# One attention block of a three-block kernel: stick-breaking weights by a running product, the band of biases loaded ahead of the norm, gates left as tanh, sliding output by two additions a step

## The chip, the cores and the metric

One Trainium2 chip, one of its cores. Time is device microseconds of that core for one execution of the whole program, the median of several runs. The trace is of one profiled execution.

## The reference, cut to what matters

Three transformer blocks follow each other on 512 tokens of width 1024. The change lies in the third block. Its two kinds of attention are:

```python
def stick_breaking_attention(q, k, v):          # 8 heads of 64
    z = jnp.einsum('bhqd,bshd->bhqs', qblk, k) * scale
    log_beta = jax.nn.log_sigmoid(z)
    log_1mb = jnp.where(causal, jax.nn.log_sigmoid(-z), 0.0)      # causal: key < query
    suffix = lax.cumsum(log_1mb, axis=3, reverse=True) - log_1mb
    a = jnp.where(causal, jnp.exp(log_beta + suffix), 0.0)
    return jnp.einsum('bhqs,bshd->bqhd', a, v)

def sliding_window_sink_attention(q, k, v, sinks, bias):   # 8 heads, 2 of keys, window 128
    s = jnp.einsum('bnqkgd,bnskd->bnkgqs', qb, kb) * scale + bias
    s = jnp.where(valid, s, -jnp.inf)
    m = jnp.maximum(jnp.max(s, axis=-1, keepdims=True), sink)
    e = jnp.exp(s - m)
    pr = e / (jnp.sum(e, axis=-1, keepdims=True) + jnp.exp(sink - m))
    return jnp.einsum('bnkgqs,bnskd->bnqkgd', pr, vb)

# third_block
h = rmsnorm(x, g_mix)
y_a = stick_breaking_attention(q_a, k_a, v_a) @ w_up_a
y_b = sliding_window_sink_attention(q_b, k_b, v_b, sinks, bias) @ w_up_b
merged = jax.nn.sigmoid(gate_a) * y_a + jax.nn.sigmoid(gate_b) * y_b
x = x + merged @ w_o
```

A stick-breaking weight is beta of its key times the product of (1 - beta) over all keys between it and the query. With r(s) the product of (1 - beta) from key s up to the query, the weight of key s is r(s + 1) - r(s); the sums over logarithms and the running product give the same weights. The bias of the sliding attention depends on the distance alone: 8 heads by 128 distances.

## The kernel before, in words

Activations lie transposed: a tile is 128 features by 512 tokens. Every large product is done in two parts of reduced precision, as three matmuls (high by high, high by low, low by high; lines 172 to 174, `gemm`). Weights come from HBM in units of 128x1024 (`wunit`, line 139): SP issues the load, ACT writes the high half (line 156, `wh`), POOL the low one (line 157, `wl`). `K.gps` gives one of the PSUM banks for such a product, and `K.sigmoid` (line 239) is a tanh on ACT and a tensor_scalar on DVE.

The third block (`block3`) runs in these stages. First the last norm of block 2 is applied to the eight tiles of X while the first three units of the block's own weights are already multiplied (`norm.head`, `norm.evict`); the evicted tiles `mb` are then scaled by the new row statistic R (L1945, L1947). Then, in program order, come the biases: two small loads (`oh`, `rb`), a matmul that picks the bias of each of 128 distances (L1992), a copy into `fr`, a row of 384 that is otherwise -1e30, a write of `fr` to DRAM and a load back (L1999) in which each partition starts one element later, so that a [128, 8, 256] band arises.

The sliding attention runs in 8 steps, 2 groups of 4 heads by 4 blocks of 128 queries. `window_scores` adds the band to the scores, takes maximum, exponential and denominator; `window_mix` transposes the weights on PE, splits them (PTh on ACT, PTl on DVE), multiplies by the values, and joins the two halves of the output, which lie in partitions 0 to 63 and 64 to 127 of PSUM, by one copy and four additions of 64x128 (L2067).

The stick-breaking attention has 8 heads. `stick_scores` computes the scores of the four query blocks of a head (128, 256, 384 and 512 keys) into PSUM, adds a mask, and forms the weights in a tile of 1280 columns: DVE clips the scores into p (L2090), ACT copies them into z (L2091), ACT takes exponential and logarithm of p (L2092, L2093), DVE the maximum with z (L2094), four scans from the last key to the first (L2097), the subtraction z - p (L2100), and ACT the exponential (L2101). `stick_mix` transposes the weights 128 columns at a time (L2110), splits them as above (L1982, L1983) and multiplies (L2112, L2113).

A string lists the order in which the pieces are traced: `ORD3[1] = "SgSMMVSSkqMSvgMSVMvSMgVSMMg"`, where S is the scores of a head, M its mix, V its values, k, q, v projections of two heads, and g a unit of gate and up-projection of the sliding output (`gate_b`). This order gives priorities. A planner at compile time orders each engine's instructions by them and by modelled durations, so a piece of lower priority is moved ahead of one whose inputs it takes for late; on the chip each engine then runs its queue in that order. After the stick stage, the gate stage (lines 2197 to 2206) multiplies the stick-breaking output and merges, and `w3_o` follows.

Of the kernel before, what the change touches and what calls it, by code (L numbers as in the profile page):

```python
# [9 lines left out]
F32 = mybir.dt.float32  # L10
# [9 lines left out]
P = 128  # L20
T = 512
# [11 lines left out]
ORD3 = ("Vkk.qqqkv", "SgSMMVSSkqMSvgMSVMvSMgVSMMg", "v")  # L33
AB = 2
DEEP3 = 1
ZP = 0
JOBS = "k0 q0 a2 v0 k1 q1 a3 v1 k2 q2 a4 v2 k3 q3 a5 v3 k4 q4 v4 k5 q5 v5 z0 g0 k6 q6 z1 v6 g1 k7 q7 z2 v7 g2 z3 g3 z4 g4 z5 g5 a6 z6 g6 a7 z7 g7"
RHP = 20
VTB = 1
# [1872 lines left out]
def block3(K, X, rms, out, norm, es):  # L1912
# [3 lines left out]
    pb = sA.enter_context(tc.tile_pool(name="b3b", bufs=8, side="right", reuse_waits="tile"))  # L1916
    mb_tile = lambda: pb.tile([P, T], F32, tag="mb", name=K.nm("mb"))
    side = Side(K, "pT3", "w3_pe", ExitStack())
    first = [(I["w3_kb"][0], P), (I["w3_vb"][0], P), (I["w3_qb"][0], P), (I["w3_qb"][1], P)][:HD[2]]
    head = [mb_tile() for _ in first]  # L1920
    if norm is not None:
# [39 lines left out]
    def proj(w, scale=None):  # L1961
        ps = K.gemm(K.gps(), gx, K.wunit(w))
        s = K.tmp()
        if scale is None:
            nc.vector.tensor_tensor(s, ps, R, MUL)
        else:
            nc.vector.scalar_tensor_tensor(s, ps, scale, R, op0=MUL, op1=MUL)
        return s
# [14 lines left out]
        nc.vector.tensor_tensor(tl, pt[:, :n], th, SUB)  # L1983
        return th, tl


    oh = pW.tile([32, P], F32, name="oh")
    nc.sync.dma_start(oh, I["onehot"])
    rb = pW.tile([32, 8], F32, name="rb")
    nc.sync.dma_start(rb, I["rel_bias"])  # L1990
    ps = K.ps("pt")
    nc.tensor.matmul(ps[:8, :P], lhsT=rb, rhs=oh, start=True, stop=True)  # L1992
    fr = pW.tile([8, 384], F32, name="fr")
    nc.gpsimd.memset(fr, NEG)
    nc.vector.tensor_copy(fr[:, 127:255], ps[:8, :P])
    scr = tc.dram_tile((8, 384), F32, name="scr")
    nc.sync.dma_start(scr, fr)
    bias = pW.tile([P, 8, 256], F32, name="bias")
    nc.sync.dma_start(bias, bass.AP(tensor=scr.tensor, offset=scr.offset, ap=[[1, P], [384, 8], [1, 256]]))  # L1999

# [49 lines left out]
    def window_mix(kv, i, A, oT):  # L2050
        k0 = max(i - 1, 0)
        nb = 2 if i else 1
        O = K.ps("o")
        for j in range(nb):
            pt = K.ps("pt")
            for h in range(4):
                nc.tensor.transpose(pt[:, h * P:(h + 1) * P], A[:, h, j * P:(j + 1) * P], K.ident)
            th, tl = to_operand(pt, T)
            V = VB[:, (k0 + j) * 2 + kv]
            nc.tensor.matmul(O, lhsT=V, rhs=th, start=j == 0, stop=False)  # L2060
            nc.tensor.matmul(O, lhsT=V, rhs=tl, start=False, stop=j == nb - 1)
        lo = pT.tile([64, T], F32, tag="lo", bufs=1, name=K.nm("lo"))
        nc.scalar.activation(lo, O[64:128], AF.Copy)
        for h in range(4):
            c = slice(h * P, (h + 1) * P)
            e = h % 2
            nc.vector.tensor_tensor(oT[h // 2][e * 64:e * 64 + 64, i * P:(i + 1) * P], O[0:64, c], lo[:, c], ADD)  # L2067

    po_tile = lambda: po.tile([P, T], F32R, tag="o", name=K.nm("oo"))


    AT_Q = {1: 0, 0: 256, 2: 384, 3: 768}

    def stick_scores(pS, q, k):
        kh, kl = k
        z = pS.tile([P, 1280], F32, tag="z", name=K.nm("z"))
        p = pS.tile([P, 1280], F32, tag="p", name=K.nm("p"))
        for blocks in ((1, 0), (2,), (3,)):
            S = K.ps("s")
            for i in blocks:  # L2080
                o = AT_Q[i] - AT_Q[blocks[0]]
                L = (i + 1) * P
                N = max(L, 256)
                ql = q[:, i * P:(i + 1) * P]
                nc.tensor.matmul(S[:, o:o + N], lhsT=ql, rhs=kh[:, :N], start=True, stop=False)
                nc.tensor.matmul(S[:, o:o + N], lhsT=ql, rhs=kl[:, :N], start=False, stop=False)
                nc.tensor.matmul(S[:, o + L - P:o + L], lhsT=K.identb, rhs=strict, start=False, stop=True)
            n = sum((i + 1) * P for i in blocks)
            c = slice(AT_Q[blocks[0]], AT_Q[blocks[0]] + n)
            nc.vector.tensor_scalar(p[:, c], S[:, :n], 40.0, None, op0=MIN)  # L2090
            nc.scalar.activation(z[:, c], S[:, :n], AF.Copy)  # L2091
        nc.scalar.activation(p, p, AF.Exp)  # L2092
        nc.scalar.activation(p, p, AF.Ln, bias=K.eps[1.0])  # L2093
        nc.vector.tensor_tensor(p, p, z, MAX)  # L2094
        for i in range(4):
            c = slice(AT_Q[i], AT_Q[i] + (i + 1) * P)
            nc.vector.tensor_tensor_scan(p[:, c][:, ::-1], K.eps[1.0].to_broadcast([P, (i + 1) * P]), p[:, c][:, ::-1], 0.0, MUL, ADD)  # L2097
        for e, a, b in ((nc.gpsimd, 0, ZP), (nc.vector, ZP, 1280)):
            if a < b:
                e.tensor_tensor(z[:, a:b], z[:, a:b], p[:, a:b], SUB)  # L2100
        nc.scalar.activation(z, z, AF.Exp)  # L2101
        return z

    def stick_mix(A, V, e, oT):
        O = K.ps("o")
# [12 lines left out]
    ob = []  # L2118
    mb = []

    def gate_b(u):
        sb = [K.sigmoid(proj(I["w3_gb"][2 * u + j])) for j in range(2)]
        w = K.wunit(I["w3_upb"][u])
        for j in range(2):
            ps = K.gemm(K.gps(), ob, w, off=j * 512)
            t = mb_tile()
            nc.vector.tensor_tensor(t, sb[j], ps, MUL)
            mb.append(t)

    q3, k3, v3, V3, Z, oa, oTs = {}, {}, {}, {}, {}, [], {}  # L2130
# [21 lines left out]
    def stick_out(h):  # L2152
        m, e = divmod(h, 2)
        if not e:
            oTs[m] = pT.tile([P, T], F32, tag="oT", bufs=2, name=K.nm("oT"))
        stick_mix(Z.pop(h), V3[m], e, oTs[m])
        if e:
            oa.append(K.split(oTs[m], None, po_tile))
# [13 lines left out]
    fill = list(ORD3[0])  # L2172
    for n, (kv, i) in enumerate(steps):
        if i == 0:
            oT = [pT.tile([P, T], F32, tag="oT", bufs=2, name=K.nm("oT")) for _ in range(2)]
        if n == 1:
            wq[1] = window_queries(1)
        if n + DEEP3 < 8:
            ahead.append(window_scores(*steps[n + DEEP3], wq[steps[n + DEEP3][0]]))
        window_mix(kv, i, ahead.pop(0), oT)  # L2180
        if i == 3:
            ob += [K.split(oT[m], None, po_tile) for m in range(2)]
        if n >= 3 and fill:
            o = fill.pop(0)
            if o != ".":
                next(todo[o])
    for o in fill:
        next(todo[o])
    sW.close()
    pS = sT.enter_context(tc.tile_pool(name="b3s", bufs=2, reuse_waits="tile"))  # L2190
    for o in ORD3[1]:
        next(todo[o])
    sT.close()
# [3 lines left out]
    for u in range(4):  # L2197
        w = K.wunit(I["w3_upa"][u], 1024, pm)
        for j in range(2):
            m = 2 * u + j  # L2200
            sa = K.sigmoid(proj(I["w3_ga"][m]))
            ps = K.gemm(K.gps(), oa, w, off=j * 512)
            t = K.tmp()
            nc.vector.tensor_tensor(t, sa, ps, MUL)
            nc.vector.tensor_tensor(t, t, mb[m], ADD)
            mg.append(K.split(t, None, lambda: pm.tile([P, T], F32R, tag="mg", bufs=16, name=K.nm("mg"))))
    rms = Rms(K, X, "g_mlp", "R4")
    for m in range(NT):
        ps = K.gemm(K.gps(), mg, K.wunit(I["w3_o"][m]))
# [78 lines left out]
```

## Time and profile before

| | us |
|---|---|
| median of 3 runs (2864.78 to 2866.42) | 2865.03 |
| the profiled execution's own time | 2863.77 |
| its span, first to last instruction | 2862.0 |
| PE busy | 2656.5 (93%) |
| DVE busy | 1764.7 (62%) |
| ACT busy | 1305.6 (46%) |
| POOL busy | 1370.3 (48%) |

The engines are PE (TensorE; PEld is its weight load), DVE (VectorE), ACT (ScalarE), POOL (GpSimd) and SP, which issues DMAs. Of the span, the third block takes what comes after about 2040 us: sliding attention to about 2156, stick-breaking attention to about 2325, the merging of the gates to 2395, then the output projection, the MLP and the side input. Engine times overlap, so a busy time is no share of the end-to-end time by itself. PEclk is the mean clock that TensorE was granted in a stretch, as a share of full speed. In a list of waits, an engine's idle time ahead of an instruction is put down to the instruction whose end released it.

### The profile page before, as it was taken

What the parts mean: (1) busy time and instruction counts of PE and PEld (TensorE: products, weight loads), DVE (VectorE), ACT (ScalarE), POOL (GpSimd) and SP (SyncE); (2) the same over time, 40 slices, a digit from 0 to 9 for tenths busy, and PEclk for the clock granted to TensorE, in tenths of its full rate; (3) what the DMA queues carried; (4) which work ended last, traced back from release to release, by engine and by line L of the source; (5) the groups of instructions that cost most, each with busy time, mean ns of one, the idle gap of its engine ahead of it and who ended that gap; (6) DMA issues with size and microseconds to landing.
All of it is one profiled execution on the core that took longest, in us unless ns stands there. A gap on an engine that the chain in (4) does not pass through costs nothing.

```text
span 2862.0 us, 34137 instructions
## 1 busy us (share of the span) xinstructions
PE 2656.5 (93%) x12206; PEld 2126.7 (74%) x12206; DVE 1764.7 (62%) x2731; ACT 1305.6 (46%) x2375; POOL 1370.3 (48%) x1049
## 2 busy tenths in 40 slices
PE   6899999699999988999989999999889799999997
PEld 5677776478888866777777788887667678788886
DVE  7889898975342496987854711136887765322256
ACT  3357776433222355666534533333556642332234
POOL 6554442454454455644536544454644344444442
PEclk9999999799999999999999999999999899999998
DMA  3321111132222222322322222232322122222222
GB/s 116 114 89 40 62 46 38 53 117 94 95 99 95 97 97 86 105 80 79 101 64 82 78 93 95 96 118 81 118 67 74 38 88 88 96 96 94 94 95 102
DMA packets 81497, 247.52 MB, mean 86 GB/s; under 512 B 11568, under 2 KB 15576, under 8 KB 81328
## 3 DMA queue, kind: packets, MB, share of 16 engines
q1 hardware_dynamic: 81328, 245.35, 26.5%
q8 instruction: 96, 1.57, 0.2%
q14 instruction: 73, 0.60, 0.1%
HBM read 233.06 MB, written 6.62 MB: 84 GB/s over the span
## 4 chain that ended last, share of the span: by engine, by line
PE 67%; DVE 22%; ACT 5%; issue 3%; DMA 1%; POOL 1%; SPq 0%; DVEq 0%; ACTq 0%; POOLq 0%
PE pg L173 19%; PE pg L172 19%; PE pg L174 19%; DVE p L2097 1%; DVE py L733 1%; DVE Zt L1543 1%; DVE X L396 1%; DVE Z L1544 1%; PE ppt L1016 1%; DMA B<-diag 1%; PE ps L994 1%; DVE ln L337 1%; POOL wl L157 1%; PE po L1022 1%; ACT wh L156 1%
## 5 line engine op out<-in xcount | busy, mean ns | idle before, releaser
L157 POOL TENSOR_TENSOR wl<-wst,wh 128x512 fp32r<-128x512 f32 (+1 forms) x808 | 1099.9, 1367 | 1312.7 <-ACT wh L156 1231.6
L156 ACT ACTIVATE wh<-wst 128x512 fp32r<-128x512 f32 (+1 forms) x808 | 500.4, 627 | 964.4 <-PE pg L173 834.9
L172 PE MATMUL pg<-op,wh 128*128 128x512 f32 (+1 forms) x2008 | 813.7, 406 | 36.4 <-ACT wh L156 19.5
L173 PE MATMUL pg<-op,wh 128*128 128x512 f32 (+1 forms) x2008 | 799.6, 398 | 6.2 <-DVE op L192 6.0
L174 PE MATMUL pg<-op,wl 128*128 128x512 f32 (+1 forms) x2008 | 798.1, 398 | 3.9 <-POOL wl L157 3.9
L172 PEld LDWEIGHTS pg<-op,wh 128*128 128x128 f32 (+1 forms) x2008 | 385.7, 192 | 115.7 <-ACT wh L156 20.2
L173 PEld LDWEIGHTS pg<-op,wh 128*128 128x128 f32 (+1 forms) x2008 | 385.5, 192 | 84.6 <-DVE op L192 8.7
L174 PEld LDWEIGHTS pg<-op,wl 128*128 128x128 f32 (+1 forms) x2008 | 384.1, 191 | 86.3 <-POOL wl L157 7.4
L172 PE MATMUL pg<-hid,wh 128*128 128x512 f32 x688 | 272.2, 396 | 0.8 <-DVE hid L191 0.8
L174 PE MATMUL pg<-hid,wl 128*128 128x512 f32 x688 | 272.2, 396 | 0.0
L173 PE MATMUL pg<-hid,wh 128*128 128x512 f32 x688 | 271.8, 395 | 0.2 <-DVE hid L192 0.2
L733 DVE SCALAR_TENSOR_TENSOR py<-z,vec,py 128x512 f32<-128x512 f32 x240 | 180.3, 751 | 10.9 <-ACT py L731 6.2
L1180 DVE TENSOR_TENSOR X<-X,pg 128x512 f32<-128x512 f32 x56 | 38.6, 689 | 222.1 <-PE pg L174 222.1
L172 PEld LDWEIGHTS pg<-hid,wh 128*128 128x128 f32 x688 | 129.1, 188 | 32.8 <-DVE hid L191 1.2
L173 PEld LDWEIGHTS pg<-hid,wh 128*128 128x128 f32 x688 | 129.1, 188 | 32.0 <-DVE hid L192 0.5
L174 PEld LDWEIGHTS pg<-hid,wl 128*128 128x128 f32 x688 | 129.1, 188 | 31.5 <-issue 0.2
L191 DVE CAST hid<-t 128x512 fp32r<-128x512 f32 x86 | 53.1, 617 | 145.5 <-ACT t L1157 144.7
L1171 DVE SCALAR_TENSOR_TENSOR t<-pg,R 128x512 f32<-128x512 f32 x32 | 22.1, 692 | 84.0 <-PE pg L174 83.9
L998 ACT ACTIVATE P<-ps,s 128x128 f32<-128x128 f32 (+3 forms) x128 | 66.5, 524 | 11.6 <-DVE s L997 9.4
L192 DVE TENSOR_TENSOR hid<-t,hid 128x512 fp32r<-128x512 f32 x86 | 63.6, 740 | 3.0
L997 DVE TENSOR_REDUCE s<-ps 128x1 f32<-128x128 f32 (+3 forms) x128 | 60.2, 483 | 8.0 <-PE ps L996 6.8
L1020 DVE TENSOR_TENSOR PTl<-ppt,PTh 128x512 fp32r<-128x512 f32 x80 | 53.4, 685 | 4.7 <-ACT PTh L1019 4.1
(546 smaller groups left out, 4420.3 us busy)
## 6 DMA issues: line engine op xcount, KB each, us to landing
wst<-in_w_f_dram SPq DMA_DIRECT2D x64, 512.0 KB
wst<-in_w_up_dram SPq DMA_DIRECT2D x32, 512.0 KB
wst<-in_w_down_dram SPq DMA_DIRECT2D x32, 512.0 KB
wst<-in_w_ga_dram SPq DMA_DIRECT2D x24, 512.0 KB
wst<-in_w_fg_dram SPq DMA_DIRECT2D x22, 512.0 KB
wst<-in_w_fu_dram SPq DMA_DIRECT2D x22, 512.0 KB
wst<-in_w_q_dram SPq DMA_DIRECT2D x16, 512.0 KB
wst<-in_w_out_dram SPq DMA_DIRECT2D x16, 512.0 KB
```

Source lines behind the costliest of these rows:

```text
L156: nc.scalar.activation(h, st, AF.Copy)
L157: nc.gpsimd.tensor_tensor(l, st, h, SUB)
L172: self.nc.tensor.matmul(ps, lhsT=wh, rhs=h[:, sl], start=first and k == 0, stop=False)
L173: self.nc.tensor.matmul(ps, lhsT=wh, rhs=l[:, sl], start=False, stop=False)
L174: self.nc.tensor.matmul(ps, lhsT=wl, rhs=h[:, sl], start=False, stop=last and k == n - 1)
L191: nc.vector.tensor_copy(h, src)
L192: nc.vector.tensor_tensor(l, src, h, SUB)
L733: nc.vector.scalar_tensor_tensor(y, z[:, k:k + T], w(k), y, op0=MUL, op1=ADD)
L997: nc.vector.tensor_reduce(mx[:, h:h + 1], S[:, :L], AX, MAX, negate=True)
L998: nc.scalar.activation(Pt[h][:, :L], S[:, :L], AF.Exp, bias=mx[:, h:h + 1], accum_out=den[:, h:h + 1])
L1020: nc.vector.tensor_tensor(tl, pt, th, SUB)
L1180: nc.vector.tensor_tensor(X[:, m], X[:, m], ps, ADD)
```

## The change

In `stick_scores`, ACT writes t = tanh(-score/2) from PSUM straight into a tile `tz`, and 0.5 + 0.5 t, which is 1 - beta, into `om`. The query blocks now lie 257, 385 and 513 columns apart in a tile of 1284: each block has one column more, where `tz` holds -1 (so `om` holds 0) and a constant tile `anew` holds 1. One scan over all columns from the last to the first computes r = om * r + anew, which starts again at 1 at each such column. The weights are the differences of neighbouring columns, one subtraction into `A`. `tz` and `om` have one buffer each, `A` has two; before, z and p had two each. The clip, the copy, the maximum, the exponentials and the logarithm are gone.

The band of biases up to its write to DRAM is moved to the top of `block3`, ahead of the norm's head, with its tiles in another pool and its product in the bank group "m". The load of the band stays where it was.

The gates stay tanh: the product with the up-projection becomes (tanh + 1) * y in one scalar_tensor_tensor, and the factor of a half goes into the split of the merged tile. In `window_mix` the output tile of a group holds two 512-column halves, and two additions of 64x(2x128) stand for four of 64x128; the stick-breaking output uses the same kind of tile.

```diff
--- before.py
+++ after.py
@@ -33,7 +33,6 @@
 ORD3 = ("Vkk.qqqkv", "SgSMMVSSkqMSvgMSVMvSMgVSMMg", "v")
-ZP = 0
...
 RHP = 20
 VTB = 1
@@ -1916,6 +1915,18 @@
     pb = sA.enter_context(tc.tile_pool(name="b3b", bufs=8, side="right", reuse_waits="tile"))
     mb_tile = lambda: pb.tile([P, T], F32, tag="mb", name=K.nm("mb"))
     side = Side(K, "pT3", "w3_pe", ExitStack())
+
+    oh = pb.tile([32, P], F32, tag="oh", bufs=1, name="oh")
+    nc.sync.dma_start(oh, I["onehot"])
+    rb = pb.tile([32, 8], F32, tag="rb", bufs=1, name="rb")
+    nc.sync.dma_start(rb, I["rel_bias"])
+    ps = K.ps("m")
+    nc.tensor.matmul(ps[:8, :P], lhsT=rb, rhs=oh, start=True, stop=True)
+    fr = pb.tile([8, 384], F32, tag="fr", bufs=1, name="fr")
+    nc.gpsimd.memset(fr, NEG)
+    nc.vector.tensor_copy(fr[:, 127:255], ps[:8, :P])
+    scr = tc.dram_tile((8, 384), F32, name="scr")
+    nc.sync.dma_start(scr, fr)
     first = [(I["w3_kb"][0], P), (I["w3_vb"][0], P), (I["w3_qb"][0], P), (I["w3_qb"][1], P)][:HD[2]]
     head = [mb_tile() for _ in first]
     if norm is not None:
@@ -1983,18 +1994,6 @@
         nc.vector.tensor_tensor(tl, pt[:, :n], th, SUB)
         return th, tl
 
-
-    oh = pW.tile([32, P], F32, name="oh")
-    nc.sync.dma_start(oh, I["onehot"])
-    rb = pW.tile([32, 8], F32, name="rb")
-    nc.sync.dma_start(rb, I["rel_bias"])
-    ps = K.ps("pt")
-    nc.tensor.matmul(ps[:8, :P], lhsT=rb, rhs=oh, start=True, stop=True)
-    fr = pW.tile([8, 384], F32, name="fr")
-    nc.gpsimd.memset(fr, NEG)
-    nc.vector.tensor_copy(fr[:, 127:255], ps[:8, :P])
-    scr = tc.dram_tile((8, 384), F32, name="scr")
-    nc.sync.dma_start(scr, fr)
     bias = pW.tile([P, 8, 256], F32, name="bias")
     nc.sync.dma_start(bias, bass.AP(tensor=scr.tensor, offset=scr.offset, ap=[[1, P], [384, 8], [1, 256]]))
 
@@ -2061,45 +2060,47 @@
             nc.tensor.matmul(O, lhsT=V, rhs=tl, start=False, stop=j == nb - 1)
         lo = pT.tile([64, T], F32, tag="lo", bufs=1, name=K.nm("lo"))
         nc.scalar.activation(lo, O[64:128], AF.Copy)
-        for h in range(4):
-            c = slice(h * P, (h + 1) * P)
-            e = h % 2
-            nc.vector.tensor_tensor(oT[h // 2][e * 64:e * 64 + 64, i * P:(i + 1) * P], O[0:64, c], lo[:, c], ADD)
+        pair = lambda t, e: t.rearrange("p (m e k) -> p m e k", m=2, e=2)[:, :, e]
+        for e in range(2):
+            nc.vector.tensor_tensor(oT[e * 64:e * 64 + 64, :, i * P:(i + 1) * P], pair(O[0:64], e), pair(lo, e), ADD)
 
     po_tile = lambda: po.tile([P, T], F32R, tag="o", name=K.nm("oo"))
 
 
-    AT_Q = {1: 0, 0: 256, 2: 384, 3: 768}
+
+    AT_Q = {1: 0, 0: 257, 2: 386, 3: 771}
+    NZ = 1284
+    ends = [AT_Q[i] + (i + 1) * P for i in range(4)]
+    anew = pT.tile([P, NZ], F32, bufs=1, name="anew")
+    nc.gpsimd.memset(anew, 0.0)
+    for c in ends:
+        nc.gpsimd.memset(anew[:, c:c + 1], 1.0)
+    half = pT.tile([P, 1], F32, bufs=1, name="half")
+    nc.gpsimd.memset(half, 0.5)
 
     def stick_scores(pS, q, k):
         kh, kl = k
-        z = pS.tile([P, 1280], F32, tag="z", name=K.nm("z"))
-        p = pS.tile([P, 1280], F32, tag="p", name=K.nm("p"))
+
         for blocks in ((1, 0), (2,), (3,)):
             S = K.ps("s")
             for i in blocks:
-                o = AT_Q[i] - AT_Q[blocks[0]]
+                o = 256 * (i == 0)
                 L = (i + 1) * P
                 N = max(L, 256)
                 ql = q[:, i * P:(i + 1) * P]
                 nc.tensor.matmul(S[:, o:o + N], lhsT=ql, rhs=kh[:, :N], start=True, stop=False)
                 nc.tensor.matmul(S[:, o:o + N], lhsT=ql, rhs=kl[:, :N], start=False, stop=False)
                 nc.tensor.matmul(S[:, o + L - P:o + L], lhsT=K.identb, rhs=strict, start=False, stop=True)
-            n = sum((i + 1) * P for i in blocks)
-            c = slice(AT_Q[blocks[0]], AT_Q[blocks[0]] + n)
-            nc.vector.tensor_scalar(p[:, c], S[:, :n], 40.0, None, op0=MIN)
-            nc.scalar.activation(z[:, c], S[:, :n], AF.Copy)
-        nc.scalar.activation(p, p, AF.Exp)
-        nc.scalar.activation(p, p, AF.Ln, bias=K.eps[1.0])
-        nc.vector.tensor_tensor(p, p, z, MAX)
-        for i in range(4):
-            c = slice(AT_Q[i], AT_Q[i] + (i + 1) * P)
-            nc.vector.tensor_tensor_scan(p[:, c][:, ::-1], K.eps[1.0].to_broadcast([P, (i + 1) * P]), p[:, c][:, ::-1], 0.0, MUL, ADD)
-        for e, a, b in ((nc.gpsimd, 0, ZP), (nc.vector, ZP, 1280)):
-            if a < b:
-                e.tensor_tensor(z[:, a:b], z[:, a:b], p[:, a:b], SUB)
-        nc.scalar.activation(z, z, AF.Exp)
-        return z
+            for i in blocks:
+                o = 256 * (i == 0)
+                L = (i + 1) * P
+                nc.scalar.activation(tz[:, AT_Q[i]:AT_Q[i] + L], S[:, o:o + L], AF.Tanh, scale=-0.5)
+        om = pS.tile([P, NZ], F32, tag="om", bufs=1, name=K.nm("om"))
+        A = pS.tile([P, NZ], F32, tag="A", name=K.nm("A"))
+        nc.scalar.activation(om, tz, AF.Identity, scale=0.5, bias=half)
+        nc.vector.tensor_tensor_scan(om[:, ::-1], om[:, ::-1], anew[:, ::-1], 0.0, MUL, ADD)
+        nc.vector.tensor_tensor(A[:, :NZ - 1], om[:, 1:], om[:, :NZ - 1], SUB)
+        return A
 
     def stick_mix(A, V, e, oT):
         O = K.ps("o")
@@ -2118,13 +2119,18 @@
     ob = []
     mb = []
 
+    def half_gate(s):
+
+        nc.scalar.activation(s, s, AF.Tanh, scale=0.5)
+        return s
+
     def gate_b(u):
-        sb = [K.sigmoid(proj(I["w3_gb"][2 * u + j])) for j in range(2)]
+        sb = [half_gate(proj(I["w3_gb"][2 * u + j])) for j in range(2)]
         w = K.wunit(I["w3_upb"][u])
         for j in range(2):
             ps = K.gemm(K.gps(), ob, w, off=j * 512)
             t = mb_tile()
-            nc.vector.tensor_tensor(t, sb[j], ps, MUL)
+            nc.vector.scalar_tensor_tensor(t, sb[j], 1.0, ps, op0=ADD, op1=MUL)
             mb.append(t)
 
     q3, k3, v3, V3, Z, oa, oTs = {}, {}, {}, {}, {}, [], {}
@@ -2152,7 +2158,9 @@
     def stick_out(h):
         m, e = divmod(h, 2)
         if not e:
-            oTs[m] = pT.tile([P, T], F32, tag="oT", bufs=2, name=K.nm("oT"))
+            if not m % 2:
+                oTs["two"] = pT.tile([P, 2, T], F32, tag="oT2", bufs=1, name=K.nm("oT"))
+            oTs[m] = oTs["two"][:, m % 2]
         stick_mix(Z.pop(h), V3[m], e, oTs[m])
         if e:
             oa.append(K.split(oTs[m], None, po_tile))
@@ -2172,14 +2180,14 @@
     fill = list(ORD3[0])
     for n, (kv, i) in enumerate(steps):
         if i == 0:
-            oT = [pT.tile([P, T], F32, tag="oT", bufs=2, name=K.nm("oT")) for _ in range(2)]
+            oT = pT.tile([P, 2, T], F32, tag="oT2", bufs=1, name=K.nm("oT"))
         if n == 1:
             wq[1] = window_queries(1)
         if n + DEEP3 < 8:
             ahead.append(window_scores(*steps[n + DEEP3], wq[steps[n + DEEP3][0]]))
         window_mix(kv, i, ahead.pop(0), oT)
         if i == 3:
-            ob += [K.split(oT[m], None, po_tile) for m in range(2)]
+            ob += [K.split(oT[:, m], None, po_tile) for m in range(2)]
         if n >= 3 and fill:
             o = fill.pop(0)
             if o != ".":
@@ -2188,6 +2196,9 @@
         next(todo[o])
     sW.close()
     pS = sT.enter_context(tc.tile_pool(name="b3s", bufs=2, reuse_waits="tile"))
+    tz = pS.tile([P, NZ], F32, bufs=1, name="tz")
+    for c in ends:
+        nc.gpsimd.memset(tz[:, c:c + 1], -1.0)
     for o in ORD3[1]:
         next(todo[o])
     sT.close()
@@ -2198,12 +2209,12 @@
         w = K.wunit(I["w3_upa"][u], 1024, pm)
         for j in range(2):
             m = 2 * u + j
-            sa = K.sigmoid(proj(I["w3_ga"][m]))
+            sa = half_gate(proj(I["w3_ga"][m]))
             ps = K.gemm(K.gps(), oa, w, off=j * 512)
             t = K.tmp()
-            nc.vector.tensor_tensor(t, sa, ps, MUL)
+            nc.vector.scalar_tensor_tensor(t, sa, 1.0, ps, op0=ADD, op1=MUL)
             nc.vector.tensor_tensor(t, t, mb[m], ADD)
-            mg.append(K.split(t, None, lambda: pm.tile([P, T], F32R, tag="mg", bufs=16, name=K.nm("mg"))))
+            mg.append(K.split(t, 0.5, lambda: pm.tile([P, T], F32R, tag="mg", bufs=16, name=K.nm("mg"))))
     rms = Rms(K, X, "g_mlp", "R4")
     for m in range(NT):
         ps = K.gemm(K.gps(), mg, K.wunit(I["w3_o"][m]))
```

## Rows read from the trace of the kernel before

**Rows 1.** The page, its head and part 1: busy us, share, instructions

```profile
span 2862.0 us, 34137 instructions
...
PE 2656.5 (93%) x12206; PEld 2126.7 (74%) x12206; DVE 1764.7 (62%) x2731; ACT 1305.6 (46%) x2375; POOL 1370.3 (48%) x1049
```

**Rows 2.** Stage table: us, length, PE, PEld, DVE, ACT, POOL busy (count), PEclk, DMA

```profile
2060.00:2100.00 40.00, 33.35 (x145) 26.18 (x144) 24.87 (x54) 17.47 (x42) 23.25 (x19) 0.87 0.36 113
2100.00:2156.00 56.00, 49.15 (x237) 36.48 (x236) 50.24 (x121) 32.44 (x89) 22.42 (x17) 1.00 0.22 67
...
2156.00:2340.00 184.00, 157.31 (x722) 124.44 (x721) 133.18 (x164) 111.97 (x164) 76.54 (x51) 0.93 0.20 63
...
2340.00:2395.00 55.00, 55.00 (x244) 45.43 (x243) 32.76 (x45) 14.96 (x26) 24.77 (x18) 1.00 0.29 96
```

**Rows 3.** Waits, 2156 to 2340 us: engine, line, releaser: total us, times, longest

```profile
POOL wl L157 <- ACT wh L156: 104.0, 23, 14.2
...
PE po L2113 <- DVE PTl L1983: 11.1, 6, 4.9
...
PE ppt L2110 <- ACT z L2101: 9.6, 4, 4.7
...
ACT z L2091 <- DVE p L2090: 8.0, 4, 4.1
...
PE ps L2085 <- ACT z L2091: 5.1, 2, 2.7
```

**Rows 4.** Groups by line, 2156 to 2340 us: busy, mean ns, idle before

```profile
L2097 DVE TENSOR_TENSOR_SCAN p<-eps,p 128x128 f32<-128x128 f32 (+3 forms) x32 | 41.0, 1342 | 0.1
L2090 DVE TENSOR_SCALAR p<-ps 128x384 f32<-128x384 f32 (+1 forms) x24 | 13.9, 594 | 9.7 <-PE ps L2087 9.7
L2091 ACT ACTIVATE z<-ps 128x384 f32<-128x384 f32 x16 | 7.3, 494 | 6.9 <-DVE p L2090 6.8
L2091 ACT ACTIVATE z<-ps 128x512 f32<-128x512 f32 x8 | 4.8, 594 | 1.3 <-DVE p L2090 1.2
L2093 ACT ACTIVATE p<-p,eps 128x1280 f32<-128x1280 f32 x8 | 10.9, 1367 | 0.1
L2093 ACT ACT_TABLE_LOAD x8 | 10.3, 1283 | 0.1
L242 ACT ACT_TABLE_LOAD x4 | 5.1, 1283 | 0.1
L2101 ACT ACT_TABLE_LOAD x4 | 5.1, 1283 | 0.1
L2101 ACT ACTIVATE z<-z 128x1280 f32<-128x1280 f32 x8 | 10.2, 1271 | 28.0 <-DVE z L2100 28.0
L2094 DVE TENSOR_TENSOR p<-p,z 128x1280 f32<-128x1280 f32 x8 | 11.9, 1490 | 9.4 <-ACT p L2093 9.4
L2100 DVE TENSOR_TENSOR z<-z,p 128x1280 f32<-128x1280 f32 x8 | 14.3, 1790 | 0.0
L244 DVE TENSOR_SCALAR t<-t 128x512 f32<-128x512 f32 x9 | 8.2, 916 | 9.4 <-ACT t L242 9.4
```

**Rows 5.** Order in time, DVE: start, us, line, form; two neighbouring heads' four scans

```profile
2230.07 3.97 DVE L2097 TENSOR_TENSOR_SCAN p<-eps,p 128x128 f32<-128x128 f32 x4
...
2246.17 7.07 DVE L2097 TENSOR_TENSOR_SCAN p<-eps,p 128x128 f32<-128x128 f32 x4
```

**Rows 6.** Order in time, 2059 to 2076 us: POOL, DVE, PE

```profile
2059.76 0.41 POOL L1994 MEMSET fr<- 8x384 f32 x1
...
2061.13 2.36 DVE L1945 TENSOR_TENSOR mb<-mb,R 128x512 f32<-128x512 f32 x2
...
2063.84 0.58 PE L1992 MATMUL ppt<-oh,rb 32*8 32x128 f32 x2 [2.88 <-DMA rb<-in_rel_bias_dram]
...
2075.41 0.42 DVE L2030 TENSOR_TENSOR A<-ps,bias 128x256 f32<-128x256 f32 x1 [2.98 <-DMA bias<-scr]
```

**Rows 7.** Groups by line, 2060 to 2156 us: the four additions of a step

```profile
L2067 DVE TENSOR_TENSOR oT<-po,lo 64x128 f32<-64x128 f32 x32 | 9.0, 282 | 2.2 <-ACT lo L2063 1.8
```

## The prediction

> **What bounds the kernel now.** I read the page's engine totals first: PE is busy 2656.5 of 2862.0 us, a share no other engine comes near [rows 1]. So a change is worth what it takes out of PE's idle time and out of the time in which PE's clock is granted low. Then the stage table (columns: stretch, its length, busy time of PE, PEld, DVE, ACT, POOL with counts, granted clock, DMA share, GB/s) finds where the touched code runs. The stick-breaking stage, 2156 to 2340 us, is 184.0 us long and PE is busy in only 157.31 of it at a mean clock of 0.93; the gate stage after it (2340 to 2395) is PE from end to end at 1.00; the two stretches ahead (2060 to 2100, 2100 to 2156) hold the band of biases and the sliding attention [rows 2]. In the stick stage PE therefore loses 184.0 - 157.31 = 26.7 us standing and, by the clock, some 0.07 x 184 = 12.9 us running in part at the lower of its two levels (1.2 and 2.4 GHz): 39.6 us is all that can be had there.
>
> The list of waits says what PE stood for [rows 3]: 11.1 us for PTl, DVE's low halves of the transposed weights; 9.6 us for the finished weights z; 5.1 us for score banks that ACT and DVE had not yet read. These three make 25.8 of the 26.7 us. The reader is to see that every one ends at DVE or ACT work of one head, and that DVE (133.18 of 184) and ACT (111.97) are far from full: it is latency in order, not throughput. The groups by line then give each instruction's price [rows 4], and the order in time shows the scans: a head's four take 3.97 us in one place and 7.07 us in another [rows 5].
>
> **The change part by part: stick_scores.** Eight heads. Removed on ACT: copies 7.3 + 4.8 us in all, two exponentials of 128x1280 a head (row of one; the other has its form) 2 x 10.2, the logarithm 10.9, and table loads 10.3 + 5.1 + 5.1 = 20.5 us, which go because tanh, identity and copy need no change of table here: tanh at L242 loads one only after a logarithm. Together 63.9 us [rows 4]. Added: four tanh a head from PSUM. A 384-wide read costs 494 ns and a 512-wide 594, so 100 ns per 128 columns, and 128 to 512 sum to 0.29 + 0.39 + 0.49 + 0.59 = 1.78 us. One identity of 1284 columns with a tile as bias, priced by the logarithm that has one too, 1.37. Eight times 3.15 is 25.2 us. ACT falls by 38.7, from 112 to 73 us.
>
> Removed on DVE: the clip 13.9, the maximum 11.9, the scans 41.0, the subtraction 14.3 us. Added: one scan of 1284 columns and one subtraction. The scan has the same two operations per element as before; its first operand is now a full tile in place of a broadcast column, a form that no row shows at this size. Bounds: 3.97 us, the undisturbed four [rows 5], and 7.07; I take the mean of before, 41.0 / 8 = 5.13. The subtraction lies between 1.49 and 1.79 (the maximum's and the old subtraction's means). So 8 x (5.13 + 1.79) = 55.3 us stand for 81.1, and nine of the gates' DVE steps (L244, 8.2 us) go in this stage: DVE falls by 34, from 133 to 99 us.
>
> Per head the chain from scores to weights was 1.27 + 1.28 + 1.37 + 1.49 + 5.13 + 1.79 + 1.27 = 13.6 us and becomes 1.37 + 5.13 + 1.79 = 8.3: shorter by 5.3, while the longest single wait for z is 4.7 [rows 3]. On PE's instructions nothing changes.
>
> What of PE's 26.7 us goes? The score banks: the slot is now given back by ACT alone, and ACT had waited 8.0 us for the clip on DVE [rows 3]; 5.1 becomes 0.5. The wait for z: in an unchanged order of PE all of it would go; but the compiler's planner writes a new order against the shorter chain and will put the transposes earlier, so I leave 3.5 of 9.6 (bounds 0 and 9.6). The wait for PTl: PTl queues on DVE behind the next head's scan, and the scan stays. The longest, 4.9, is the one behind the 7.07 us scan and I cut it to 2.0; the other 6.2 I leave at 5.5. So 7.5 of 11.1 (bounds 3 and 11.1). With 0.6 of small ones PE stands 12.1 us, 14.6 less. The low clock follows standing in this stage, 12.9 / 26.7 = 0.48 us per us: 7.1 more. Stage: -21.7 us. What is late next is PTl behind the scan.
>
> On that scan the trace shows 3.97 us where POOL runs little and 7.07 where POOL's splits run beside it [rows 5]. The Trainium skill, SBUF — State Buffer, section Who interferes with whom, says that a DVE instruction with two SBUF inputs and a GpSimd instruction that reads SBUF exclude each other for a whole instruction. By that rule one long scan is held off once rather than up to four times, so its price is nearer the lower bound, and DVE would save up to 8 x 1.16 = 9.3 us more, which is mostly off the path; it also means that POOL is held for a whole scan, which is the last rival below.
>
> **The gates.** Sixteen tensor_scalar steps on DVE go; the factor of a half moves into the split of the merged tile, and the added one rides on the product that reads PSUM anyway. In the gate stage PE has no gap [rows 2], so this is worth nothing there; in the stick stage it is counted above. Were the products dearer by as much as the removed step (0.92), that would give back 8 us of DVE's 34 and still be covered by DVE's idle time.
>
> **The band of biases.** PE stands 2.88 us for its two small loads and then runs the 0.58 us product; but the transposes behind it need the second of two evicted tiles, ready at 2061.13 + 2.36 = 2063.49, only 0.35 before that product starts at 2063.84 [rows 6]. So the old place yields 0.35 + 0.58 us, not 3.4, and the product's 0.58 is paid again where it goes. All of it is issued again ahead of the norm: two loads, a write to DRAM and the memset pass the queues of SP and POOL there, the product and a copy those of PE and DVE. The write waits on SP for the copy, with the next weight loads queued behind it. If PE stood for the loads there as it does here, 2.9 is lost. DVE's 2.98 us wait for the band at 2075.41 goes [rows 6], but DVE is busy only 24.87 of 40 us in that stretch [rows 2]. I take -0.5 (bounds -2.9 and +2.6).
>
> **The sliding output.** 32 additions of 0.282 [rows 7] become 16 of 256 columns; the 256-column addition out of PSUM takes 0.42 [rows 6]: 9.0 becomes 6.7, in a stretch where DVE is busy 50.24 of 56 us and PE 49.15. Of the 2.3 us I take 1.0 on the path (bounds 0 and 2.3). **New memsets:** ten on POOL, one of 1284 columns; by the 384-column one, 0.41 [rows 6], 1.4 us and at most 0.41 for each other. Six of them, 3.4 us, fall where POOL is busy 23.25 of 40 [rows 2]; I take +0.5 (bounds 0 and 3.4).
>
> **Sum.** -21.7 - 0.5 - 1.0 + 0.5 = -22.7 from the profiled execution's 2863.77 (span 2862.0 and 1.77 around it): 2841.1. The median shown, 2865.03, lies 1.26 above it, so 2842.
>
> **Rivals.** *PE runs dense.* For it: DVE at 99 and ACT at 73 us are far under PE's 157. Against: the order on PE is fixed when the kernel is built and the scan stays. All 39.6 and 1.5 elsewhere go: 2824. *Only the banks.* The new plan pulls the transposes ahead as far as the chain got shorter, and the waits for z and PTl stay: 4.6 x 1.48 = 6.8 and 1.0 elsewhere: 2857. *It doesn't save what it says:* the plan gives back every gap, or the scan over two full tiles costs what the removed steps did (81.1 / 8 = 10.1 us a head less the subtraction's 1.79, so a scan of 8.3): 2865. *The single om buffer, slower.* om was two tiles p; now the identity of a head waits for the subtraction of the head before, and behind it on ACT's queue stand the splits of weights, PTh and tanh, for which PE waits. Held for scan and subtraction, 5.5 us, on seven heads, it costs 7 x 5.5 x 1.48 = 57: 2899; it turns the result above the old time from 22.7 / 1.48 / 7 = 2.2 us a head. It decides if two heads' scores come less than 5.5 us apart; before, two neighbours' scans start 16.1 apart [rows 5]. *POOL held by the long scan.* Weight splits come up to 3.97 us later for each of eight heads: 8 x 3.97 x 1.48 = 47, so 2889; against it, POOL idles 104.0 us of this stage waiting for ACT [rows 3], and PE's large waits name no split.
>
> **How the numbers follow.** Forecast 0.55 (its own range 2832 to 2852), dense 0.14, only the banks 0.15, nothing saved 0.08, om 0.05, POOL 0.03. About 0.2% (5.7 us) is what can be told from no change: faster 0.55 + 0.14 + 0.15 = 0.84, same 0.08, slower 0.08. The range, 2822 to 2859, takes in the first three.
>
> **What would show it.** Right: no table load between 2156 us and the stage's end, one scan a head of 4 to 5.5 us, the stage near 162 us, PE's longest wait there PTl behind a scan, next to none for score banks. Wrong: waits for A above 6 us in sum (the plan), a scan above 7 us with POOL idle, ACT waiting for DVE ahead of the identity, or PE waiting for wl.

## The result, and the profile after

The changed kernel takes 2834.23 us (median of 4 runs, 2831.8 to 2839.88) against 2865.33 us: the ratio is 0.9895 (95% interval 0.9881 to 0.991). On another chip, beside the last experiments, it was 0.992 (0.9901 to 0.9939), 2838.68 against 2862.52 us. So the change is worth 24 to 31 us, and the forecast, 2842 us with 22.7 us taken off, lies just under that. Single runs of one kernel lay up to 20 us apart (the band alone: 2854.22 to 2873.77; the kernel before on that chip: 2854.99 to 2869.82), so differences under some 4 us between experiments are not read.

The profiled execution of the changed kernel is the fastest of the first four, 2831.8 us, and 6.0 us of its lead over the profile of before had arisen by the last addition of block 2 (1947.0 and 1953.0 us), before the first instruction that the edits move or add (2003.9). Over all fourteen profiles of this case that addition starts anywhere from 1946.4 to 1958.9 us. Stages are therefore compared by their lengths. From the first column sum of the third block's norm to the first addition of the output projection the kernel before needs 344.8 us (2052.7 to 2397.5) and the changed one 316.6 (2048.5 to 2365.1), 28.2 less. What follows takes 464.5 and 464.9 us. This stretch leaves out what the moved band costs ahead of the column sum (below). Counted from the last addition of block 2, the kernel before needs 444.46 us up to the same end and the changed one 418.13, 26.33 less. The change's lines are one less than before up to the third block, so L156 here is L157 there.

The page's head and part 1 of the changed kernel, to set against [rows 1]:

```profile
span 2830.0 us, 34046 instructions
...
PE 2644.3 (93%) x12206; PEld 2119.3 (75%) x12206; DVE 1712.2 (61%) x2643; ACT 1269.2 (45%) x2351; POOL 1366.0 (48%) x1059
```

The stage table, its borders moved to the same pieces of work (columns as in [rows 2]):

```profile
2055.00:2095.00 40.00, 33.30 (x147) 26.48 (x146) 24.98 (x51) 18.23 (x43) 24.14 (x19) 0.87 0.32 103
2095.00:2150.00 55.00, 47.73 (x233) 35.90 (x232) 49.37 (x107) 31.80 (x87) 23.07 (x21) 1.00 0.23 68
2150.00:2306.00 156.00, 146.82 (x716) 116.03 (x715) 86.55 (x98) 75.68 (x140) 76.28 (x51) 0.99 0.24 75
2306.00:2361.00 55.00, 55.00 (x244) 45.45 (x243) 27.64 (x36) 14.47 (x25) 24.20 (x18) 1.00 0.28 95
```

The stick stage is 156 us long in place of 184. PE stands 9.2 us of it, not 26.7, and its clock is granted at 0.99, not 0.93. The stages ahead of it and the gate stage are as long as they were. The waits of PE and ACT between 2150 and 2325 us (columns as in [rows 3]):

```profile
PE po L2114 <- DVE PTl L1994: 5.9, 6, 2.9
...
PE po L2113 <- DVE VA L1988: 1.9, 1, 1.9
...
ACT om L2100 <- DVE A L2102: 1.3, 2, 1.0
...
PE po L2113 <- DVE oT L2117: 0.6, 1, 0.6
PE ps L2091 <- ACT tz L2097: 0.5, 1, 0.5
```

The wait of PE for finished weights is gone, that for score banks is 0.5, and that for PTl is about halved. The groups of the new instructions (columns as in [rows 4]; there is no table load among them):

```profile
L2101 DVE TENSOR_TENSOR_SCAN om<-om,anew 128x1284 f32<-128x1284 f32 x8 | 23.4, 2922 | 9.3 <-ACT om L2100 9.3
L2102 DVE TENSOR_TENSOR A<-om 128x1283 f32<-128x1283 f32 x8 | 16.7, 2092 | 0.1
L2100 ACT ACTIVATE om<-tz,half 128x1284 f32<-128x1284 f32 x8 | 11.0, 1373 | 1.4 <-DVE A L2102 1.3
...
L2133 DVE SCALAR_TENSOR_TENSOR mb<-t,pg 128x512 f32<-128x512 f32 x8 | 5.5, 688 | 16.9 <-PE pg L173 16.9
...
L2097 ACT ACTIVATE tz<-ps 128x512 f32<-128x512 f32 x8 | 4.7, 590 | 1.7 <-PE ps L2093 1.6
```

One scan takes 2.92 us in the mean, where four took 5.13 [rows 4]. The band of biases, in the order in time of DVE and PE (compare [rows 6]):

```profile
2056.74 2.31 DVE L1956 TENSOR_TENSOR mb<-mb,R 128x512 f32<-128x512 f32 x2
...
2059.20 1.09 PE L1985 MATMUL ppt<-ident,mb 128*128 128x128 f32 x4 [3.59 <-DVE mb L1956]
...
2069.12 0.41 DVE L2029 TENSOR_TENSOR A<-ps,bias 128x256 f32<-128x256 f32 x1
```

DVE no longer waits for the band, and PE no longer for its loads; PE now stands 3.59 us at the same place for the evicted tiles. Counted from the column sum (2052.66 and 2048.50 us), the transposes there start 1.0 us earlier, at 10.70 us in place of 11.70. But time is lost ahead of the column sum. From the last addition of block 2 to it the changed kernel needs 101.5 us, the kernel before 99.6. The waits of PE in that part, first in the changed kernel and then before (columns as in [rows 3]):

```profile
PE pg L171 <- ACT o L1805: 2.9, 1, 2.9
PE pg L171 <- DVE ln L431: 2.7, 1, 2.7
PE pm L412 <- POOL wl L156: 1.3, 1, 1.3
```

```profile
PE pm L413 <- POOL wl L157: 3.3, 1, 3.3
PE pg L172 <- DVE ln L432: 0.9, 1, 0.9
```

The wait of 2.9 us for `o`, a copy out of PSUM by ACT, stands in the traces of all six kernels that have the band moved, which need 100.4 to 102.6 us there. It stands in none of the eight others, which need 99.6 to 99.8. How the moved instructions bring it about was not taken apart.

### The profile page after: what moved, and what is told of

Read it like the earlier page. It is cut to its first block, busy times and chain, and to the rows that moved or that the text cites. A ratio compares the mean times of both kernels' runs of the same rounds, so it can differ in the third digit from the quotient of the medians.

```text
span 2830.0 us, 34046 instructions
## 1 busy us (share of the span) xinstructions
PE 2644.3 (93%) x12206; PEld 2119.3 (75%) x12206; DVE 1712.2 (61%) x2643; ACT 1269.2 (45%) x2351; POOL 1366.0 (48%) x1059
## 4 chain that ended last, share of the span: by engine, by line
PE 70%; DVE 19%; ACT 5%; issue 2%; POOL 1%; DMA 1%; SPq 0%; DVEq 0%; ACTq 0%; POOLq 0%
PE pg L172 20%; PE pg L171 20%; PE pg L173 20%; DVE py L732 1%; DVE Zt L1542 1%; DVE Z L1543 1%; PE ppt L1015 1%; DVE X L395 1%; PE piv L1568 1%; PE ps L993 1%; DVE ln L336 1%; POOL wl L156 1%; PE po L1021 1%; ACT wh L155 1%; ACT P L997 1%
## 5 line engine op out<-in xcount | busy, mean ns | idle before, releaser
L156 POOL TENSOR_TENSOR wl<-wst,wh 128x512 fp32r<-128x512 f32 (+1 forms) x808 | 1094.1, 1360 | 1277.4 <-ACT wh L155 1201.1
```

The source lines that it names most:

```text
L156: nc.gpsimd.tensor_tensor(l, st, h, SUB)
```

## The experiments

All ran beside the kernel before; "stretch" is the one of 344.8 us above, from each kernel's own profile, and the last column counts from the last addition of block 2, as the 444.46 us above. Ratios are to the kernel before of the same chip: the first four rows are from one chip, the next four from a second, the last four from a third.

| | ratio (95% interval) | stretch, us | from block 2, us |
|---|---|---|---|
| stick_scores alone | 0.9914 (0.9897 to 0.9932) | 318.3 | 417.9 |
| band alone | 1.0005 (0.9992 to 1.0019) | 340.6 | 441.6 |
| gates alone | 0.9982 (0.997 to 0.9995) | 336.5 | 436.2 |
| two additions alone | 1.0009 (0.9999 to 1.0018) | 341.8 | 441.6 |
| before, one scan | 0.9962 (0.9947 to 0.9977) | 335.8 | 435.5 |
| changed, table loads back | 0.9913 (0.9899 to 0.9927) | 318.8 | 419.2 |
| before, gates in place | 0.9998 (0.9987 to 1.0009) | 342.0 | 441.7 |
| stick_scores and gates | 0.9919 (0.9906 to 0.9933) | 317.0 | 416.8 |
| changed again | 0.992 (0.9901 to 0.9939) | 313.6 | 416.2 |
| changed, no two additions | 0.9917 (0.9898 to 0.9936) | 316.7 | 418.2 |
| changed, band in its old place | 0.9915 (0.9898 to 0.9931) | 318.0 | 417.6 |
| changed, four scans | 0.9928 (0.991 to 0.9946) | 323.0 | 424.2 |

Three kernels whose time is that of the kernel before (band alone, two additions alone, gates in place) need 441.6 to 441.7 us from block 2 on, 2.7 to 2.9 less than the one profile of the kernel before. So some 3 us of the 26.33 are owed to that profile, and the 24 us of the third chip are the better figure for the change.

**Each edit alone.** Each of the first four takes one part of the diff shown above onto the kernel before.

> The kernel before with the new stick_scores alone (tanh, one scan, one subtraction). Theory (the shorter chain of a head takes PE's waits away): 24 to 28 us under the kernel before, near 2839, the stage from 2156 us on about 24 us shorter, no table load in it. Rival (the gain needs DVE's relief by the gates and the two additions too): at most 15 us, above 2850.

> The kernel before with the band of biases moved ahead of the norm, alone. Theory: PE's wait for the two loads was almost wholly hidden by the wait for the evicted tiles behind it, so 0 to 2 us faster. Rival (the wait of 2.9 us and DVE's wait of 3.0 us for the band were both on the path): 3 to 6 us faster. Other rival (queues ahead of the norm): slower by 1 us or more.

> The kernel before with the gates left as tanh, alone. Theory: nothing in the gate stage, where PE has no gap, and up to 2 us in the stick stage, where nine steps of 0.9 us leave DVE's queue: 0 to 2 us faster. Rival (DVE's queue is the bound of the stick stage): 5 us or more faster.

> The kernel before with two additions a step and the two-half output tile, alone. Theory: 1 us faster (0 to 2.3). Rival (one buffer in place of two holds the next group back): slower by 1 us or more.

stick_scores alone is 24.4 us faster (2838.53 against 2862.97), inside what its theory expected: the gain needs no other edit. The band and the two additions show nothing; the additions' 1 us of the forecast can't be seen, and at 1.0009 their interval leaves 0.3 us of gain at most. The gates alone are 5.1 us faster (2857.91), more than the theory's 2, though the interval (1.4 to 8.6 us) reaches down into it. In their trace the wait for PTl is as before, that for z is 10.7 us against 9.6, and only that for score banks has gone, from 5.1 to 0.6 us (waits of PE, columns as in [rows 3]):

```profile
PE po L2113 <- DVE PTl L1983: 11.1, 6, 4.9
PE ppt L2110 <- ACT z L2101: 10.7, 3, 4.8
PE ps L2085 <- ACT z L2091: 0.6, 2, 0.3
```

**Why the gates help alone.** Two causes were possible, fewer steps on DVE or fewer temporary tiles. The second was tried by itself:

```diff
-        sb = [K.sigmoid(proj(I["w3_gb"][2 * u + j])) for j in range(2)]
+        # gate(s): tanh and tensor_scalar both in place
+        sb = [gate(proj(I["w3_gb"][2 * u + j])) for j in range(2)]
```

> The kernel before with the gates' tanh and tensor_scalar done in place, so that a gate holds one temporary tile and not two; DVE's step stays. Theory (temporary tiles were scarce): 3 to 6 us faster, as the gates left as tanh. Rival (DVE's sixteen steps were the gain): no change within 2 us.

At 0.9998 the tiles give nothing that can be seen (the interval leaves 3.7 us at most). What is left is DVE's sixteen steps, which fits the wait for banks that went but was not tried by itself. On top of stick_scores the gates give nothing (0.9919 with, 0.9914 without, on two chips): with stick_scores alone the wait for banks is already 0.5 us.

**What in stick_scores: the scan.** The kernel before with one scan per head, all else as it was:

```diff
-        for i in range(4):
-            c = slice(AT_Q[i], AT_Q[i] + (i + 1) * P)
-            nc.vector.tensor_tensor_scan(p[:, c][:, ::-1], K.eps[1.0].to_broadcast([P, (i + 1) * P]), p[:, c][:, ::-1], 0.0, MUL, ADD)
+        nc.vector.tensor_tensor_scan(p[:, ::-1], keep[:, ::-1], p[:, ::-1], 0.0, MUL, ADD)   # keep: 1, and 0 at each block's end
```

> The kernel before with its four scans of a head made one of 1280 columns, reset at the block ends by a tile of ones and zeros; clip, logarithm, maximum and exponentials stay. Theory A (a scan is held off by at most one POOL instruction of about 1 us, so four pay up to four times): the scan 2.8 to 3.6 us in place of a mean of 5.1, DVE 12 to 18 us less in the stage, and 6 to 12 us faster. Theory B (the gain comes from the ACT part of the chain): the scan is as short, but at most 4 us faster.

It is 11.3 us faster (2851.45 against 2862.76; interval 6.6 to 15.2 us): theory A. The scan's durations (ns, least, median, greatest) beside those of before, of all widths:

```profile
L2100 DVE TENSOR_TENSOR_SCAN p<-keep,p x8: 2815/3418/3906, 2177.0 to 2306.4; 128x1280 f32<-128x1280 f32 x8
```

```profile
L2097 DVE TENSOR_TENSOR_SCAN p<-eps,p x32: 415/1192/2276, 2172.3 to 2314.5; 128x128 f32<-128x128 f32 x8, 128x256 f32<-128x256 f32 x8, 128x384 f32<-128x384 f32 x8, 128x512 f32<-128x512 f32 x8
```

Why, is seen in the kernel before scan by scan, first the head of 2230 us and then that of 2246, of which [rows 5] gives the lengths (there the four records overlap by some 0.08 us each, so singly they add up to more). In time the order is 128, 256, 384, 512 columns; the lists are sorted by duration:

```profile
L2097 DVE TENSOR_TENSOR_SCAN p<-eps,p 128x128 f32<-128x128 f32 x1 | 1.4, 1427 | 0.0
L2097 DVE TENSOR_TENSOR_SCAN p<-eps,p 128x512 f32<-128x512 f32 x1 | 1.2, 1191 | 0.0
L2097 DVE TENSOR_TENSOR_SCAN p<-eps,p 128x384 f32<-128x384 f32 x1 | 0.9, 926 | 0.0
L2097 DVE TENSOR_TENSOR_SCAN p<-eps,p 128x256 f32<-128x256 f32 x1 | 0.7, 659 | 0.0
```

```profile
L2097 DVE TENSOR_TENSOR_SCAN p<-eps,p 128x512 f32<-128x512 f32 x1 | 2.2, 2223 | 0.0
L2097 DVE TENSOR_TENSOR_SCAN p<-eps,p 128x384 f32<-128x384 f32 x1 | 2.0, 1978 | 0.0
L2097 DVE TENSOR_TENSOR_SCAN p<-eps,p 128x256 f32<-128x256 f32 x1 | 1.7, 1712 | 0.0
L2097 DVE TENSOR_TENSOR_SCAN p<-eps,p 128x128 f32<-128x128 f32 x1 | 1.4, 1386 | 0.0
```

What POOL did meanwhile (start, us, instruction):

```profile
2229.93 1.29 POOL L157 TENSOR_TENSOR wl<-wst,wh 128x512 fp32r<-128x512 f32 x1 [5.35 <-ACT wh L156]
2233.25 1.87 POOL L157 TENSOR_TENSOR wl<-wst,wh 128x512 fp32r<-128x512 f32 x1 [2.03 <-ACT wh L156]
...
2245.97 2.67 POOL L157 TENSOR_TENSOR wl<-wst,wh 128x512 fp32r<-128x512 f32 x2 [7.00 <-ACT wh L156]
2248.85 3.30 POOL L157 TENSOR_TENSOR wl<-wst,wh 128x512 fp32r<-128x512 f32 x2 [0.21 <-ACT wh L156]
```

At 2230.07 one split on POOL is running as the first scan starts, and that scan is long; no split runs as the other three start. At 2246 each of the four scans starts while a split runs, and all four are long. So it is for all 32 scans of this trace. The 14 that start with no POOL instruction running are still (415, 659, 926, 1191 ns for 128 to 512 columns at the shortest). The 18 that start while one runs are longer, 15 of them by 0.97 to 1.09 us (2223 - 1191 = 1032, 1978 - 926 = 1052, 1712 - 659 = 1053, 1386 - 415 = 971) and three by 0.50 to 0.63. In all 18 the excess is the rest of the running POOL instruction, less 0.11 to 0.14 us. So a scan is not slowed, it is held off until that instruction ends, whatever its own width. Four scans can pay four times, and one pays once. POOL is held in turn: a split of 1.29 us beside a still DVE takes 1.87 us when it starts during a scan, as at 2233.25, and up to 3.7 us beside the scan of the changed kernel.

**The scan from the other side.** The changed kernel with its scan cut in four over the same tiles:

```diff
-        nc.vector.tensor_tensor_scan(om[:, ::-1], om[:, ::-1], anew[:, ::-1], 0.0, MUL, ADD)
+        for i in range(4):
+            c = slice(AT_Q[i], ends[i] + 1)
+            nc.vector.tensor_tensor_scan(om[:, c][:, ::-1], om[:, c][:, ::-1], anew[:, c][:, ::-1], 0.0, MUL, ADD)
```

> The changed kernel with its one scan of a head cut into four of 129 to 513 columns over the same two tiles. Theory A (each scan is held off by a POOL instruction of its own): the four take 3.2 us where POOL is still and up to 7 where it runs, 4 to 5 in the mean in place of 2.9, and PE's wait for PTl grows; 4 to 10 us slower than the changed kernel. Rival (the full tile as first operand is what is fast): 3.2 to 3.4 in the mean, within 3 us.

```profile
L2103 DVE TENSOR_TENSOR_SCAN om<-om,anew 128x513 f32<-128x513 f32 x8 | 11.7, 1462 | 0.0
L2103 DVE TENSOR_TENSOR_SCAN om<-om,anew 128x385 f32<-128x385 f32 x8 | 9.6, 1198 | 0.0
L2103 DVE TENSOR_TENSOR_SCAN om<-om,anew 128x257 f32<-128x257 f32 x8 | 6.4, 798 | 0.0
L2103 DVE TENSOR_TENSOR_SCAN om<-om,anew 128x129 f32<-128x129 f32 x8 | 5.2, 651 | 10.1 <-ACT om L2100 10.1
```

The mean of four is 32.9 / 8 = 4.1 us, theory A's lower edge; the full tile as first operand is not what makes it fast. Seven of the 32 scans are held off here, 18 of 32 in the kernel before. One more starts while POOL has a split under way and is not held off: that split began during the scan just ahead and ended 1.1 us after this one, so it was the split that waited. The stretch is 323.0 us, 6 to 9 more than the two profiles of the changed kernel. PE's wait for PTl hardly grows (6.5 us), that for VA does (3.8). By the runs it is 4.1 us slower than the changed kernel (2842.77 and 2838.68), theory A's lower edge again, but the intervals overlap: the profiles support the sign, the size is open.

**What in stick_scores: the table loads.** The changed kernel with two loads ahead of each head's identity:

```diff
+        K.table("natural_log_exp_and_others")
+        K.table("exp_and_others")
         nc.scalar.activation(om, tz, AF.Identity, scale=0.5, bias=half)
```

> The changed kernel with two table loads ahead of the identity of each head: 16 x 1.28 = 20.5 us of ACT back, in the chain of a head. Theory B (ACT's part of the chain): 6 to 14 us slower than the changed kernel, 16 to 24 under the kernel before. Rival (PE is now covered by other work): within 4 us of the changed kernel.

The waits of PE in the same part of its trace:

```profile
PE po L2116 <- DVE PTl L1994: 7.9, 6, 3.9
PE pg L173 <- POOL wl L156: 1.0, 1, 1.0
PE po L2115 <- DVE oT L2119: 0.8, 1, 0.8
PE po L2115 <- ACT PTh L1993: 0.7, 2, 0.4
```

With all 20.5 us of ACT back the ratio is 0.9913; the changed kernel's was 0.9895 on the first chip and 0.992 beside the later experiments. Stick_scores with the gates, on the same chip as this run, has 0.9919. The stretch grows by 2 to 5 us, and no wait for finished stick weights returns. So in the changed kernel the loads cost little, and theory B (ACT's part of the chain) falls for them there. What taking them out was worth in the kernel before, whose chain is longer, no run shows.

**Undoing the rest.** Stick_scores with the gates alone had come out at 0.9919, which against the first chip's 0.9895 looked as if the band and the additions were worth 7 us after all. So the changed kernel was run again, on a third chip, beside versions without the one and without the other.

> The changed kernel without the moved band and without the two additions: stick_scores and gates alone. Theory (the other two edits give nothing): within 4 us of the changed kernel, near 2833 to 2838. Rival (each gives its predicted 0.5 and 1.0 or more, in combination): 2 to 5 us slower than the changed kernel.

> The changed kernel again, on the same chip as the three beside it, as their measure: 0.987 to 0.991 of the kernel before.

> The changed kernel without the two additions a step and the two-half tile. Theory (alone they gave nothing, so they give nothing here): within 3 us of the changed kernel. Rival (they help once the stick stage is short, which would explain why stick_scores and gates without them and without the band came out at 0.992): 3 to 8 us slower than the changed kernel.

> The changed kernel with the band of biases in its old place. Theory (the wait for the loads is hidden by the evicted tiles): within 3 us of the changed kernel. Rival (the band is the missing part of the gain): 3 to 8 us slower.

The changed kernel itself is at 0.992 there, above the 0.987 to 0.991 that was expected. The two beside it have 0.9915 and 0.9917, stick_scores with the gates had 0.9919. So nothing was missing: the edits do not differ. What stands apart is the first chip's 0.9895, and as its interval (to 0.991) just overlaps that of 0.992 (from 0.9901), whether chip or chance made it is open.

## Why the prediction was right, step by step

*PE's gaps in the stick stage are what can be had* held: the stage fell by 28 us by the profiles, where 21.7 was forecast, and stick_scores alone brings all that the runs show (24.4 us). *The wait for score banks, 5.1 to 0.5*: measured 0.5. *The wait for PTl, 11.1 to 7.5*: 5.9, and the longest, 2.9 us at 2201.7 to 2204.6, stands behind a subtraction of 2.59 us, not behind a scan. *The wait for weights, 9.6 to 3.5*: none; the fear that the planner's new order would bring it back was not borne out. PE stands 9.2 us where 12.1 was forecast, with 2.5 of it on two new waits (VA and oT) that were not foreseen. The clock followed: 0.01 of 156 us is lost, under 2 us, where 5.8 was left.

*ACT to 73 us* was 75.7 in the stage, with tanh (590 ns at 512 columns, forecast 594) and identity (1.373, forecast 1.37) as priced by their neighbours. *DVE to 99* was 86.6, and here a term was mis-sized: the scan. I read the four scans of 3.97 us as undisturbed and took them for the lower bound; they hold one wait of 1.0 us, as the rows above show, so the undisturbed four take some 2.96. One scan of 1284 columns takes 2.83 at best, below my bound, and 2.92 in the mean where I took 5.13; the sign "one scan a head of 4 to 5.5 us" failed with it. The Trainium skill's rule (SBUF — State Buffer, Who interferes with whom), which I weighed and put aside, says that a DVE instruction with two SBUF inputs contends with a GpSimd instruction that reads SBUF, and that the shared ports are an exclusive lock; the trace agrees, as all 18 scans that were held off waited for the end of a POOL instruction. By that rule I had the new scan nearer the lower bound of 3.97; it came out below it. The one-scan experiment puts that term at 11.3 us of end time in the kernel before, so it is the largest part of the gain that was measured by itself, and the forecast named it only as mostly off the path. In the changed kernel, four scans again cost 4.1 us, a size that is open. How the rest divides between DVE's clip and maximum and ACT's copies, logarithm and exponentials was not separated; of it only the table loads were tried, and in the changed kernel alone. The forecast took PE's waits off by judgement, for a shorter chain, and gave the scan no gain at all; that it came within 1 to 8 us all the same is partly luck.

*The subtraction, 1.49 to 1.79*: 2.09, dearer, by the same holding off: the one that starts with POOL still takes 1.48, the other seven 0.22 to 1.11 us more.

*The band*: the reason given (the evicted tiles hide the loads) is what the trace shows: the wait of 2.88 became one of 3.59 for the tiles, and the place yields 1.0 us, close to the 0.35 + 0.58 of the sum. What the sum had too small is the price ahead of the norm: 0.7 to 3.0 us are lost there, with a new wait of 2.9 us, so nothing was gained where I took 0.5. *The memsets*, priced at 0.5 us, cost nothing that shows: three kernels that have them and not the moved band need 99.7 to 99.8 us ahead of the column sum, as the kernel before does with 99.6. *The two additions* take 6.6 us in all (forecast 6.7) and gain nothing that can be measured, where I took 1.0: DVE's 2.3 us were not on the path. *The gates* were right as part of the whole (nothing on top of stick_scores); as an edit alone they gave more than the theory of that run, 5.1 us. Their products are hardly dearer: 688 ns in the mean, against 671 to 687 before.

*The rivals.* PE did not run dense: of the 39.6 us that it lost in the stage before, 28 went, between the forecast's 21.7 and all of it. The om buffer cost ACT 1.3 us in two waits. POOL, held by the long scan, cost PE nothing: no wait of PE for wl is in the list. The waits were not given back by the plan.

## What to carry to other kernels

Look at instructions one by one, beside what the other engines run at that moment, before taking a sum of them as undisturbed. Where an instruction is longer each time another engine's instruction runs at its start, by the rest of that one, it is held off; this is paid per instruction, and merging the four scans took most of it away. A wait that vanishes is worth only what the next release leaves over: the band's loads were hidden by tiles that came 0.35 us earlier. What is moved out of a stage is to be looked for where it went: a stretch that starts behind that place makes the move look like a gain. Undo every part of a composite change on one chip before summing parts measured on different ones.

## What the runs showed of the hardware that was not expected

A tensor_tensor_scan of 128x1284 in fp32 takes 2.83 us, 2.2 ns per column, and a broadcast column or a full tile as its first operand makes no difference (at the shortest, 415, 659, 926 and 1191 ns for 128 to 512 columns over the broadcast column; 426, 661, 927 and 1192 for 129 to 513 over the full tile). In the kernel before each of the 18 scans that start while a POOL instruction runs is held off until that one ends, by 0.50 to 1.09 us, whatever its width, and its record is longer by as much; a split on POOL that runs into a long scan takes up to 3.7 us in place of 1.29. And 20.5 us of table loads put back into ACT's queue of the changed kernel moved the end time by no more than the measurement can tell.
